# One 128-key, 64-query score matmul per chunk in HGRN2's six lower levels, in place of two of 64 by 32

## The chip, the cores and the metric

The kernel runs on one core of a Trainium2 chip. The metric is device time of one execution in microseconds (us). Three runs of the kernel before took 2519.35, 2517.97 and 2510.12 us, median 2517.97. The execution that the profiler recorded took 2514.51 us, of which the trace spans 2512.7.

## The reference

One decoder layer over 2048 tokens of width 1024, in float32: RMSNorm, one wide input projection, three token mixers, gates, an output projection, a residual and a final norm. Only mixer A, HGRN2, is touched. It has 4 heads of 128 key and 128 value channels, and works in chunks of 64 tokens. Within a chunk

```
b = jnp.cumsum(gb, axis=2)
diff = b[:, :, :, None, :] - b[:, :, None, :, :]
decay = jnp.exp(jnp.where(causal, diff, -jnp.inf))
scores = jnp.einsum('bhtk,bhsk,bhtsk->bhts', qb, kb, decay)
o = (jnp.einsum('bhts,bhsv->bhtv', scores, vb)
     + jnp.einsum('bhtk,bhkv->bhtv', qb * jnp.exp(b), state))
```

The decay between key s and query t differs for each of the 128 channels, so the scores are not one plain product of Q and K.

## The kernel before

The tokens are taken in four blocks of 512 (`block`, s = 0 to 3), each of which is four chunks of 128 tokens in this kernel (`NT` = 4, indexed c). A block projects the normed tokens onto all columns of `w_in`: every float32 product is written as three matmuls of 128x512 (L101, L102, L103; high times high, high times low, low times high), with weights streamed from DRAM. In the first block the weights are also split into high and low parts (L86 on ScalarE, L87 on VectorE) and kept in DRAM; later blocks load the kept parts. Around these projections the mixers run: `unit_a(h)` for each of 4 HGRN2 heads, `unit_b` for DeltaNet, `unit_c` for attention, and `merge` for each branch.

`unit_a` builds the decayed scores by levels. Tokens of a chunk are rows 0 to 127. At level lv (0 to 6) the chunk falls into blocks of 2h tokens, h = 2^lv, and each block into a lower and an upper half. The scores between queries of upper halves and keys of lower halves of the same block are exact products of Q and K as they stand at this level. After that Q of the upper halves is multiplied by the decay total of the lower half (L411), and K of the lower halves by that of the upper half (L412); so Q and K are right for the next level. A level's steps are these:

- TensorE: the score matmuls of the four chunks into one PSUM bank `sp` (L402 for levels 0 to 5, L406 for level 6). They read Q and K.
- VectorE: L411 writes Q and L412 writes K in place, so both wait for the score matmuls, and the matmuls of the next level wait for both.
- VectorE: L415 copies from `sp` to the score tile `SD` where the mask `amask` of this level is set (copy_predicated). `SD` has 128 rows (keys) by 64 columns (queries of the same 64-token half) for each chunk.
- GpSimd: L425 multiplies pairs of decay totals for the next level.

Queries and keys in different 64-token halves of a chunk meet only at level 6 (L406). So levels 0 to 5 need, for each chunk, two 64 by 64 squares, and of each only the 32 queries in upper halves. Before, each square has a matmul of its own: 64 keys are the stationary operand (64 columns of the array), 32 queries stream, and `tile_position=(0, g * 64)` puts the half g into columns 64g to 64g + 63 of the array and partitions 64g to 64g + 63 of the bank. A level has 8 such calls; each float32 call shows in the trace as two weight loads and two matmuls, so a level is 16 and the kernel (4 blocks, 4 heads, 6 levels: 96 groups) is 1536.

L406 (level 6) also uses a column tile, and is not changed. After level 6 the score tile goes to `ST` (L421, L422 on ScalarE), L429 and L434 are transposes, and L444 to L446 apply the scores and the state. L338 are transposes of the head before (`y_gate`), which fall among the first levels of the next head. L121 is the last step of a SiLU (`gate_ct`), on VectorE.

The instructions of an engine run in the order of its program. A scheduler lays the engines' programs out ahead of the run: it sets the projection matmuls (L101 to L103) between the score groups of two levels. PSUM banks for scores come from a pool of two per head parity (`bank(ct)`).

Of the kernel before, what the change touches and what calls it, by code (L numbers as in the profile page):

```python
# [20 lines left out]
P = 128  # L21
# [3 lines left out]
NT = TB // P  # L25
# [26 lines left out]
def _trunk(tc, S, a, out):  # L52
# [9 lines left out]
    V, A, G, T = nc.vector, nc.scalar, nc.gpsimd, nc.tensor  # L62
# [9 lines left out]
    def bank(tag="d", w=None):  # L72
        return ps.tile([P, 512], F32, name="ps_" + tag, tag=tag, bufs=4 if tag == "d" else 2)
# [44 lines left out]
    def silu2(dst, src, tag="tr"):  # L118
        th = sb.tile([P, src.shape[-1]], F32, name="th", tag=tag, bufs=2)
        last_act[0] = A.activation(th, src, AF.Tanh, scale=0.5).ins  # L120
        V.scalar_tensor_tensor(dst, th, 1.0, src, op0=ALU.add, op1=ALU.mult)  # L121
# [93 lines left out]
    amask = const.tile([P, 6, 32], U8, name="amask", tag="amask")  # L215
# [25 lines left out]
    def row_scale(so, c, eps):  # L241
        G.tensor_tensor(so[:, c:c + 1], so[:, c:c + 1], eps, op=ALU.add)
        G.tensor_tensor(so[:, c:c + 1], so[:, c:c + 1], mhalf4[:, 0:1], op=ALU.pow)
# [70 lines left out]
    def block(s, hH, hL, last=None):  # L314
        t0 = s * TB

        def proj_ct(idx):
            p = bank()
            mm_ct(p, a["wct"][idx], hH, hL, KT)
            return p  # L320

        def gate_ct(idx):
            pg = proj_ct(idx)
            gt = sb.tile([P, TB], F32, name="gt", tag="gt")
            silu2(gt, pg)
            return gt
# [5 lines left out]
        def y_gate(o, so, gt, nw, ct):  # L332
            pt = bank(ct)
            with tc.issue_after(last_act[0]), tc.issue_after(last_mm[0]):
                for c in range(NT):
                    A.activation(o[:, c, :], o[:, c, :], AF.Copy, scale=so[:, c:c + 1])
                for c in range(NT):
                    T.transpose(pt[:, c * P:(c + 1) * P], o[:, c, :], ident)  # L338
            V.scalar_tensor_tensor(gt, pt, nw, gt, op0=ALU.mult, op1=ALU.mult)

        def y_split(yT, h, gt):
            A.copy(yT[0][:, h, :], gt)  # L342
            V.tensor_tensor(yT[1][:, h, :], gt, yT[0][:, h, :].bitcast(F32), op=ALU.subtract)  # L343
# [25 lines left out]
        def unit_a(h):  # L369
            ct = "c%d" % (h % 2)  # L370
            hs = slice(h * P, (h + 1) * P)
            qk = sb.tile([P, 2, TB], F32, name="qk", tag="qk")
            Q, K = qk[:, 0, :], qk[:, 1, :]
            pf = proj_ct(4 + h)
            F = sb.tile([P, TB], F32, name="F", tag="w0")
            A.activation(F, pf, AF.Sigmoid)
            A.activation(K, pf, AF.Sigmoid, scale=-1.0)
            A.activation(F, F, AF.Identity, scale=omlb[:, h:h + 1], bias=lb[:, h:h + 1])
            A.activation(K, K, AF.Copy, scale=omlb[:, h:h + 1])
            pq = proj_ct(h)  # L380
            silu2(Q, pq)
            gt = gate_ct(8 + h)
            prod = sb.tile([P, TB], F32, name="prod", tag="w1")
            G.tensor_tensor(prod, Q, K, op=ALU.mult)
            V.tensor_tensor(Q, Q, F, op=ALU.mult)
            ST = sb.tile([P, NT, P], F32, name="ST", tag="w2")
            G.memset(ST[64:P, :, 0:64], 0.0)
            SD = sb.tile([P, NT, 64], F32, name="SD", tag="xf")
            G.memset(SD, 0.0)
            tots = sb.tile([P, TB], F32, name="tots", tag="w3")  # L390
            tot = F
            off = 0
            for lv in range(7):
                hh = 1 << lv
                nb = 64 >> lv
                v5 = lambda t: t.rearrange("p (c b two h) -> p c b two h", c=NT, b=nb, two=2, h=hh)
                sp = bank(ct)
                qv, kv = v5(Q), v5(K)
                for c in range(NT):
                    if lv < 6:  # L400
                        for g in range(2):
                            T.matmul(sp[g * 64:g * 64 + 64, c * 32:(c + 1) * 32], K[:, c * P + g * 64:c * P + g * 64 + 64],  # L402
                                     qv[:, c, g * nb // 2:(g + 1) * nb // 2, 1, :], start=True, stop=True,
                                     tile_position=(0, g * 64))
                    else:
                        T.matmul(sp[0:64, c * 64:(c + 1) * 64], kv[:, c, 0, 0, :], qv[:, c, 0, 1, :],  # L406
                                 start=True, stop=True, tile_position=(0, 0))
                tv = tot.rearrange("p (c b two) -> p c b two", c=NT, two=2)
                te = tv[:, :, :, 0:1].broadcast_to([P, NT, nb, hh])
                to = tv[:, :, :, 1:2].broadcast_to([P, NT, nb, hh])  # L410
                V.tensor_tensor(qv[:, :, :, 1, :], qv[:, :, :, 1, :], te, op=ALU.mult)  # L411
                V.tensor_tensor(kv[:, :, :, 0, :], kv[:, :, :, 0, :], to, op=ALU.mult)  # L412
                if lv < 6:
                    n2 = nb // 2
                    V.copy_predicated(  # L415
                        SD.rearrange("p c (b two h) -> p c b two h", b=n2, two=2, h=hh)[:, :, :, 1, :],
                        amask[:, lv, :].rearrange("p (o b h) -> p o b h", o=1, b=n2).broadcast_to([P, NT, n2, hh]),
                        sp[:, :P].rearrange("p (c b h) -> p c b h", c=NT, b=n2))
                else:
                    for r in (0, 64):  # L420
                        A.copy(ST[r:r + 64, :, r:r + 64], SD[r:r + 64])  # L421
                    A.copy(ST[0:64, :, 64:P], sp[0:64, 0:256].rearrange("p (c h) -> p c h", c=NT))  # L422
                nt_ = tots[:, off:off + NT * nb]
                off += NT * nb
                G.tensor_tensor(nt_.rearrange("p (c b) -> p c b", c=NT), tv[:, :, :, 0], tv[:, :, :, 1], op=ALU.mult)  # L425
                tot = nt_
            cp = bank(ct)
            for c in range(NT):
                T.transpose(cp[:, c * P:(c + 1) * P], prod[:, c * P:(c + 1) * P], ident)  # L429
            cc = sb.tile([P, NT], F32, name="cc", tag="cc")  # L430
            V.tensor_reduce(cc, b3(cp), axis=mybir.AxisListType.X, op=ALU.add)
            kp = bank(ct)
            for c in range(NT):
                T.transpose(kp[:, c * P:(c + 1) * P], K[:, c * P:(c + 1) * P], ident)  # L434
            KTt = sb.tile([P, TB], F32, name="KTt", tag="w4")
            A.copy(KTt, kp)
            o = b3(prod)
            st = stA[h]
            so = sb.tile([P, NT], F32, name="so", tag="so")
            for c in range(NT):  # L440
                cs = slice(c * P, (c + 1) * P)
                op = bank(ct)
                vv = vA[:, c, hs]
                T.matmul(op[:, 0:P], ST[:, c, :], vv, start=True, stop=False)  # L444
                T.matmul(op[:, 0:P], Q[:, cs], st, start=False, stop=True)
                T.matmul(op[:, P:2 * P], KTt[:, cs], vv, start=True, stop=True)  # L446
                V.scalar_tensor_tensor(st, st, tot[:, c:c + 1], op[:, P:2 * P], op0=ALU.mult, op1=ALU.add)
                V.scalar_tensor_tensor(o[:, c, :], vv, cc[:, c:c + 1], op[:, 0:P], op0=ALU.mult, op1=ALU.add)
                junk = sb.tile([P, P], BF16, name="junk", tag="junk")
                A.activation(junk, o[:, c, :], AF.Square, accum_out=so[:, c:c + 1])  # L450
                row_scale(so, c, epsa)

            def fin(yT):
                y_gate(o, so, gt, norma, ct)
                y_split(yT, h, gt)
            return fin
# [317 lines left out]
        if last:  # L774
            last()
        yA = new_y()
        f0 = unit_a(0)
        if s == 0:
            bias_rows()
        f1 = unit_a(1)  # L780
        if s == 0:
            bias_spread()
        f0(yA)
        proj_k()
        f2 = unit_a(2)
        if s == 0:
            bias_load()
# [126 lines left out]
```

## Time and profile before

| what | value |
|---|---|
| runs (median; lowest to highest) | 2517.97 us; 2510.12 to 2519.35 |
| profiled execution | 2514.51 us, span 2512.7 us |
| TensorE matmul busy | 97% of the span, 13658 matmuls |
| VectorE, ScalarE, GpSimd busy | 47%, 35%, 17% |
| granted TensorE clock, mean | 0.984 |
| DMA queues' share of 16 engines | 55% for the main one |

Busy is the time in which at least one instruction of the engine is in progress. Consecutive matmuls overlap: one takes about 0.39 us from its start to its end, and the next starts before that. So the pace is read from the differences of starts, not from durations. A weight load (PEld) is an instruction of its own, and runs beside matmuls.

### The profile page before, as it was taken

To read this page: it belongs to the slowest core of one execution; us is meant where nothing else is said; L and a number is where in the kernel's file an instruction comes from. 1 tells how busy PE (TensorE), PEld (TensorE's weight loads), DVE (VectorE), ACT (ScalarE), POOL (GpSimd) and SP (SyncE) were. 2 spreads that over 40 slices of the span, in tenths; PEclk is the share of its full clock that TensorE was granted. 3 is DMA by queue.
4 is the path that set the end of the run, shared out by engine and by line. 5 is a ranking of instruction groups with operands and counts; after the bars stand their busy time and mean duration, and the time that the engine had idled before them with its cause. 6 is when DMAs were issued, how large, how long until landed. Compare 5 with 4: busy or idle time off the path is not lost. (4 is left out here: it accounts for less than half of the span.)

```text
span 2512.7 us, 37478 instructions
## 1 busy us (share of the span) xinstructions
PE 2428.6 (97%) x13658; PEld 1946.4 (77%) x13658; DVE 1170.9 (47%) x3188; ACT 869.2 (35%) x2288; POOL 434.2 (17%) x821
## 2 busy tenths in 40 slices
PE   8999998999999999899999999989999999998998
PEld 7777776778877777678887877767888787876886
DVE  5666575465345535524214553551322455455321
ACT  5454344444334313323223422332322342233221
POOL 3221011211222101111112210111111221111111
PEclk9999998999999999999999999999999999999999
DMA  7756673769944455264774455425566354442555
GB/s 244 247 193 224 221 260 96 241 221 336 299 134 130 154 161 158 83 208 148 247 218 127 139 156 165 146 88 193 167 228 210 122 155 149 160 150 87 176 193 175
DMA packets 193156, 452.84 MB, mean 180 GB/s; under 512 B 52243, under 2 KB 70588, under 8 KB 192844
## 3 DMA queue, kind: packets, MB, share of 16 engines
q1 hardware_dynamic: 192972, 450.45, 55.3%
q8 instruction: 108, 1.77, 0.3%
q14 instruction: 76, 0.62, 0.1%
HBM read 348.81 MB, written 103.14 MB: 180 GB/s over the span
## 5 line engine op out<-in xcount | busy, mean ns | idle before, releaser
L101 PE MATMUL ps_d<-hH,wHL 128*128 128x512 f32 x1952 | 785.6, 402 | 4.1 <-DVE mm L700 2.2
L102 PE MATMUL ps_d<-hL,wHL 128*128 128x512 f32 x1952 | 783.5, 401 | 0.0
L103 PE MATMUL ps_d<-hH,wHL 128*128 128x512 f32 x1952 | 779.9, 400 | 0.7 <-DVE wHL L87 0.7
L101 PEld LDWEIGHTS ps_d<-hH,wHL 128*128 128x128 f32 x1952 | 369.4, 189 | 77.5 <-DVE mm L700 3.9
L103 PEld LDWEIGHTS ps_d<-hH,wHL 128*128 128x128 f32 x1952 | 369.3, 189 | 71.8 <-issue 1.8
L102 PEld LDWEIGHTS ps_d<-hL,wHL 128*128 128x128 f32 x1952 | 369.4, 189 | 68.0 <-issue 1.7
L87 DVE TENSOR_TENSOR wHL<-wraw,wHL 128x512 fp32r<-128x512 f32 (+1 forms) x194 | 130.6, 677 | 93.3 <-ACT wHL L86 91.2
L362 POOL TENSOR_TENSOR msum<-msum,gth 128x512 f32<-128x512 f32 x64 | 88.6, 1387 | 443.6 <-DVE gth L361 443.6
L101 PE MATMUL ps_d<-yH,wHL 128*128 128x512 f32 x384 | 155.3, 406 | 5.8 <-ACT yH L342 3.7
L86 ACT CAST wHL<-wraw 128x512 fp32r<-128x512 f32 (+1 forms) x194 | 113.7, 590 | 130.9 <-PE ps_d L103 80.8
L103 PE MATMUL ps_d<-yH,wHL 128*128 128x512 f32 x384 | 154.9, 403 | 0.0
L102 PE MATMUL ps_d<-yL,wHL 128*128 128x512 f32 x384 | 153.8, 401 | 0.1
L352 ACT ACTIVATE gth<-ps_d 128x512 f32<-128x512 f32 x96 | 57.3, 597 | 256.9 <-PE ps_d L103 256.1
L361 DVE SCALAR_TENSOR_TENSOR gth<-gth,ps_d 128x512 f32<-128x512 f32 x64 | 43.9, 687 | 184.9 <-PE ps_d L103 177.4
L169 PE MATMUL ps_d<-wHL,mH 128*128 128x512 f32 x256 | 99.7, 391 | 1.3 <-DMA wHL<-kept 1.3
L502 DVE SCALAR_TENSOR_TENSOR qkB<-raw,convw,qkB 128x512 f32<-128x512 f32 x96 | 71.7, 746 | 61.2 <-ACT qkB L500 59.9
L170 PE MATMUL ps_d<-wHL,mH 128*128 128x512 f32 x256 | 99.6, 389 | 0.0
L171 PE MATMUL ps_d<-wHL,mL 128*128 128x512 f32 x256 | 99.5, 389 | 0.0
L101 PEld LDWEIGHTS ps_d<-yH,wHL 128*128 128x128 f32 x384 | 73.0, 191 | 21.8 <-ACT yH L342 4.6
L102 PEld LDWEIGHTS ps_d<-yL,wHL 128*128 128x128 f32 x384 | 73.6, 192 | 15.9 <-DVE yL L343 1.7
L103 PEld LDWEIGHTS ps_d<-yH,wHL 128*128 128x128 f32 x384 | 73.5, 191 | 15.2 <-issue 0.5
L402 PEld LDWEIGHTS ps_c<-qk 128*64 128x64 f32 x1536 | 52.6, 137 | 33.3 <-issue 20.4
(281 smaller groups left out, 3761.0 us busy)
## 6 DMA issues: line engine op xcount, KB each, us to landing
wHL<-kept SPq DMA_DIRECT2D x486, 512.0 KB, 3.6
kept<-wHL SPq DMA_DIRECT2D x162, 512.0 KB, 4.0
wraw<-in_wct_dram SPq DMA_DIRECT2D x122, 256.0 KB, 3.7
wHL<-kept SPq DMA_DIRECT2D x32, 324.0 KB, 4.1
xT<-in_xT_dram SPq DMA_DIRECT2D x32, 256.0 KB, 4.6
xs<-in_x_dram SPq DMA_DIRECT2D x32, 256.0 KB, 4.4
rt<-in_x_dram SPq DMA_DIRECT2D x32, 256.0 KB, 4.6
out_dram<-rt SPq DMA_DIRECT2D x32, 256.0 KB, 4.0
```

Source lines behind the costliest of these rows:

```text
L86: A.copy(w[:, 0, :n], raw[:, :n])
L87: V.tensor_tensor(w[:, 1, :n], raw[:, :n], w[:, 0, :n].bitcast(F32), op=ALU.subtract)
L101: T.matmul(p, wh[:, ks], rh[kt], start=(kt == 0), stop=False)
L102: T.matmul(p, wh[:, ks], rl[kt], start=False, stop=False)
L103: last_mm[0] = T.matmul(p, wl[:, ks], rh[kt], start=False, stop=(kt == nk - 1)).ins
L169: T.matmul(pj[j][:, :n], lh[kt][:, js], wh, start=(kt == 0), stop=False)
L170: T.matmul(pj[j][:, :n], lh[kt][:, js], wl, start=False, stop=False)
L171: T.matmul(pj[j][:, :n], ll[kt][:, js], wh, start=False, stop=(kt == KT - 1))
L352: A.activation(th, gp, AF.Tanh, scale=0.5)
L362: G.tensor_tensor(m, m, th, op=ALU.add)
L402: T.matmul(sp[g * 64:g * 64 + 64, c * 32:(c + 1) * 32], K[:, c * P + g * 64:c * P + g * 64 + 64], qv[:, c, g * nb // 2:(g + 1) * nb // 2, ...
L502: V.scalar_tensor_tensor(dst, raw[:, j:j + TB], convw[:, ti, j:j + 1], dst, op0=ALU.mult, op1=ALU.add)
```

## The change

For levels 0 to 5 each chunk has one score matmul: all 128 keys are the stationary operand (128 columns of the array, no column tile), and the 64 queries of upper halves of both 64-token halves stream. The bank then also holds products of keys of one half and queries of the other, which nothing reads. A level has 4 calls, 8 weight loads and 8 matmuls; `sp` uses 256 columns instead of 128. As the wanted columns differ between the two partition halves, L415 becomes two predicated copies of 64 partitions each. Level 6 is unchanged.

```diff
                 for c in range(NT):
                     if lv < 6:
-                        for g in range(2):
-                            T.matmul(sp[g * 64:g * 64 + 64, c * 32:(c + 1) * 32], K[:, c * P + g * 64:c * P + g * 64 + 64],
-                                     qv[:, c, g * nb // 2:(g + 1) * nb // 2, 1, :], start=True, stop=True,
-                                     tile_position=(0, g * 64))
+                        T.matmul(sp[:, c * 64:(c + 1) * 64], K[:, c * P:(c + 1) * P], qv[:, c, :, 1, :],
+                                 start=True, stop=True)
                     else:
...
                 if lv < 6:
                     n2 = nb // 2
-                    V.copy_predicated(
-                        SD.rearrange("p c (b two h) -> p c b two h", b=n2, two=2, h=hh)[:, :, :, 1, :],
-                        amask[:, lv, :].rearrange("p (o b h) -> p o b h", o=1, b=n2).broadcast_to([P, NT, n2, hh]),
-                        sp[:, :P].rearrange("p (c b h) -> p c b h", c=NT, b=n2))
+                    for r in (0, 64):
+                        V.copy_predicated(
+                            SD[r:r + 64].rearrange("p c (b two h) -> p c b two h", b=n2, two=2, h=hh)[:, :, :, 1, :],
+                            amask[r:r + 64, lv, :].rearrange("p (o b h) -> p o b h", o=1, b=n2).broadcast_to([64, NT, n2, hh]),
+                            sp[r:r + 64, 0:256].rearrange("p (c g b h) -> p g c b h", c=NT, g=2, b=n2)[:, r // 64])
```

In the changed file the lines after the edit move: its L401 is the score matmul (before L402), L409 and L410 are the updates of Q and K (before L411, L412), L414 the predicated copies (before L415), and L404 the level-6 matmul (before L406).

TensorE's program in the third block, head 0, levels 2 to 4, before (`ps_d` is a projection's bank, `ps_c` with a number one level's score bank, `wHL` streamed weights, `hH` and `hL` the normed tokens' parts, `qk` the tile of Q and K; xN is the number of calls):

```order
L402 MATMUL ps_c_12284<-qk 64x32 x8
L103 MATMUL ps_d<-hH,wHL 128x512
L101 MATMUL ps_d<-hH,wHL 128x512
L102 MATMUL ps_d<-hL,wHL 128x512
L103 MATMUL ps_d<-hH,wHL 128x512
L402 MATMUL ps_c_12297<-qk 64x32 x8
L101 MATMUL ps_d<-hH,wHL 128x512
```

and with the change:

```order
L401 MATMUL ps_c_12134<-qk 128x64 x4
L103 MATMUL ps_d<-hH,wHL 128x512
L101 MATMUL ps_d<-hH,wHL 128x512
L102 MATMUL ps_d<-hL,wHL 128x512
L103 MATMUL ps_d<-hH,wHL 128x512
L401 MATMUL ps_c_12144<-qk 128x64 x4
L101 MATMUL ps_d<-hH,wHL 128x512
```

Here nothing but the group itself changes: four projection matmuls stand between two levels, as before.

VectorE's program at the same place, before (`tots` are the decay totals, `SD` the scores):

```order
L411 TENSOR_TENSOR qk<-qk,tots 128x32x8
L412 TENSOR_TENSOR qk<-qk,tots 128x32x8
L415 COPY_PREDICATED SD<-amask,ps_c_12297 128x16x8
L411 TENSOR_TENSOR qk<-qk,tots 128x16x16
```

and with the change:

```order
L409 TENSOR_TENSOR qk<-qk,tots 128x32x8
L410 TENSOR_TENSOR qk<-qk,tots 128x32x8
L414 COPY_PREDICATED SD<-amask,ps_c_12144 64x16x8 x2
L409 TENSOR_TENSOR qk<-qk,tots 128x16x16
```

The second copy stands behind the updates of Q and K, and ahead of those of the next level.

TensorE's program between levels 0 and 1 of head 1 in the third block, before (L338 are the transposes of head 0's output):

```order
L402 MATMUL ps_c_12510<-qk 64x32 x8
L101 MATMUL ps_d<-hH,wHL 128x512
L102 MATMUL ps_d<-hL,wHL 128x512
L103 MATMUL ps_d<-hH,wHL 128x512
L338 MATMUL ps_c_12654<-ident,prod 128x128
L101 MATMUL ps_d<-hH,wHL 128x512
L338 MATMUL ps_c_12654<-ident,prod 128x128
L102 MATMUL ps_d<-hL,wHL 128x512
L338 MATMUL ps_c_12654<-ident,prod 128x128
L103 MATMUL ps_d<-hH,wHL 128x512
L402 MATMUL ps_c_12523<-qk 64x32 x8
L338 MATMUL ps_c_12654<-ident,prod 128x128
```

and with the change:

```order
L401 MATMUL ps_c_12348<-qk 128x64 x4
L101 MATMUL ps_d<-hH,wHL 128x512
L102 MATMUL ps_d<-hL,wHL 128x512
L103 MATMUL ps_d<-hH,wHL 128x512
L338 MATMUL ps_c_12474<-ident,prod 128x128 x2
L101 MATMUL ps_d<-hH,wHL 128x512
L338 MATMUL ps_c_12474<-ident,prod 128x128
L102 MATMUL ps_d<-hL,wHL 128x512
L338 MATMUL ps_c_12474<-ident,prod 128x128
L401 MATMUL ps_c_12358<-qk 128x64 x4
```

All four transposes now stand ahead of the level-1 group, and one projection matmul fewer.

## Rows read from the trace of the kernel before

**Rows 1.** The page: span, busy time of each engine.

```profile
span 2512.7 us, 37478 instructions
PE 2428.6 (97%) x13658; PEld 1946.4 (77%) x13658; DVE 1170.9 (47%) x3188; ACT 869.2 (35%) x2288; POOL 434.2 (17%) x821
```

**Rows 2.** One line, L402: durations (min/median/max, ns), and its waits.

```profile
L402 PEld LDWEIGHTS ps_c<-qk x1536: 132/138/139, 62.9 to 2029.0; 128*64 128x64 f32 x192
L402 PE MATMUL ps_c<-qk x1536: 222/223/244, 62.9 to 2029.1; 128*64 128x32 f32 x192
  DVE qk L411: 83.4, 90
```

**Rows 3.** Timeline of PE (start, duration), third block: 21 projection matmuls, first and last.

```profile
1308.77 0.39 PE L101 MATMUL ps_d<-hH,wHL 128*128 128x512 f32 x1
...
1313.30 0.39 PE L103 MATMUL ps_d<-hH,wHL 128*128 128x512 f32 x1
```

**Rows 4.** Timeline of PE, third block, head 0, levels 1 to 3.

```profile
1316.02 0.66 PE L402 MATMUL ps_c<-qk 128*64 128x32 f32 x16
...
1317.41 0.39 PE L102 MATMUL ps_d<-hL,wHL 128*128 128x512 f32 x1
1317.73 0.66 PE L402 MATMUL ps_c<-qk 128*64 128x32 f32 x16
...
1319.45 0.66 PE L402 MATMUL ps_c<-qk 128*64 128x32 f32 x16
```

**Rows 5.** Timeline of PE and PEld, end of the same head: groups without column tiles.

```profile
1329.17 0.40 PE L445 MATMUL ps_c<-stA,qk 128*128 128x128 f32 x2
...
1331.47 0.41 PE L445 MATMUL ps_c<-stA,qk 128*128 128x128 f32 x2
...
1330.67 0.30 PEld L444 LDWEIGHTS ps_c<-vA,ST 128*128 128x128 f32 x2
1330.89 0.19 PEld L102 LDWEIGHTS ps_d<-hL,wHL 128*128 128x128 f32 x1
```

**Rows 6.** Timeline of PE, third block: 128-column weights with 16 streamed columns.

```profile
1404.16 0.29 PE L480 MATMUL ps_c<-gg,triu 128*128 128x16 f32 x2
1404.52 0.63 PE L338 MATMUL ps_c<-ident,prod 128*128 128x128 f32 x4
```

**Rows 7.** Timeline, third block, head 0, level 6 and its first users.

```profile
1324.59 0.68 PE L406 MATMUL ps_c<-qk 128*64 128x64 f32 x8
1324.97 0.81 ACT L421 COPY ST<-SD 64x256 f32<-64x256 f32 x2
...
1326.92 0.38 PE L444 MATMUL ps_c<-vA,ST 128*128 128x128 f32 x2
```

**Rows 8.** Timeline of DVE at levels 2 and 3 of rows 4.

```profile
1318.44 0.42 DVE L411 TENSOR_TENSOR qk<-qk,tots 128x256 f32<-128x256 f32 x1 [0.60 <-PE ps_c L402]
1318.78 0.42 DVE L412 TENSOR_TENSOR qk<-qk,tots 128x256 f32<-128x256 f32 x1
1319.12 0.28 DVE L415 COPY_PREDICATED SD<-amask,ps_c 128x128 f32<-128x128 uint8 x1
```

**Rows 9.** Timeline of DVE and PEld, DeltaNet: a load that waits for VectorE.

```profile
2291.61 0.35 DVE L642 TENSOR_SCALAR vn<-ps_c,cols 128x128 f32<-128x128 f32 x1 [0.22 <-PE ps_c L640]
2292.01 0.30 PEld L644 LDWEIGHTS ps_c<-vn,KD 128*128 128x128 f32 x2 [0.18 <-DVE vn L642]
```

**Rows 10.** Timeline of DVE, head 1, level 0.

```profile
1340.24 0.43 DVE L411 TENSOR_TENSOR qk<-qk,F 128x256 f32<-128x256 f32 x1 [2.62 <-PE ps_c L402]
...
1341.18 0.42 DVE L412 TENSOR_TENSOR qk<-qk,F 128x256 f32<-128x256 f32 x1
```

**Rows 11.** Groups by line, shapes apart (busy us, mean ns, idle before).

```profile
L415 DVE COPY_PREDICATED SD<-amask,ps_c 128x128 f32<-128x128 uint8 x96 | 32.6, 339 | 0.0
L666 DVE TENSOR_TENSOR kL<-ps_d,kH 64x512 fp32r<-64x512 f32 x16 | 11.0, 687 | 0.4
L750 DVE TENSOR_TENSOR rt<-ps_d,rt 128x512 f32<-128x512 f32 x32 | 21.4, 688 | 81.8 <-PE ps_d L171 81.8
```

## The prediction

> **What bounds the kernel.** I read the page's busy shares first, then the changed line by itself, then the order of time around it on TensorE and on VectorE. TensorE is busy for 97% of the span, the next engine for 47% [rows 1]. What lengthens or shortens TensorE's program by itself therefore moves the end by as much; what happens on VectorE counts only where TensorE comes to wait for it. The reader should see in the line's own rows that the busy time is no price: 1536 matmuls of 223 ns lie over one another, and the rows do not say what a group costs [rows 2]. The price is in the starts.
>
> **What a group costs now.** A projection matmul follows the one before in (1313.30 - 1308.77) / 20 = 0.2265 us [rows 3]. From one score group to the next with four of them between it is (1319.45 - 1316.02) / 2 = 1.715 us [rows 4]. So a group takes 1.715 - 4 x 0.2265 = 0.81 us of TensorE. Its 16 matmuls start within 0.66 - 0.223 = 0.44 us of each other, 29 ns apart on the mean; the other 0.37 us is entry and exit. At the entry the group starts 0.32 us after the projection matmul ahead of it (1317.73 - 1317.41) [rows 4], where 0.2265 would do: some 0.09 us are lost before a column tile. The rest is lost behind it.
>
> The Trainium skill says the same of the entry ("TensorEngine Tiling (Array Packing)", Key Properties): to change the tiling mode drains the engine. The 0.09 us agrees with that, and the change does away with it.
>
> **What a group will cost.** There are 8 matmuls, each with a load of 128 columns, no column tile, and 64 streamed columns. No row before has just this. Three rows lie around it.
>
> - With 128-column loads and 128 streamed columns: between two L445 stand six matmuls of L445, L446 and L444 and two projections, and (1331.47 - 1329.17) / 2 - 2 x 0.2265 = 0.70 us for six, 0.116 each with entry and exit. The loads alone follow each other at 1330.89 - 1330.67 = 0.22 us for two, 0.11 each [rows 5]. For 8: 0.88 by the loads, 0.93 by the whole.
> - With 128-column loads and only 16 streamed columns: four matmuls of L480 and L481 take 1404.52 - 1404.16 = 0.36 us, 0.09 each [rows 6]. For 8: 0.72. So short streams hardly help: the load sets the pace.
> - With 64-column loads and 64 streamed columns: one matmul's 0.222 taken off, (0.68 - 0.222) / 7 = 0.065 each [rows 2, 7]. For 8 with 0.03 at the ends: 0.55.
>
> I take 0.90, since the loads of 128 columns are what all rows with such loads are paced by, and the nearest group in length (six) gives 0.116 with its ends. Per group 0.90 - 0.81 = +0.09 us, and 96 groups make **+8.6 us**. The bounds are 0.72 (-8.6 us) and 0.93 (+11.5 us). In words: half as many matmuls, but two loads of 64 columns, one in each half of the array, go through in 2 x 29 = 58 ns, and one load of 128 takes 110. What the mode switches give back (0.3 us a group) is a little less than what the loads cost.
>
> The Trainium skill has a rule that speaks against the change too ("TensorE: Matmul & The Clock Gate", LDWEIGHTS (loading the stationary operand)): the time of a load goes with its columns, about one per 1.2 GHz cycle, so 107 ns for 128. The load rows agree (0.11). By that figure 8 loads take 0.86 us, and the term would be +5 us instead of +8.6.
>
> **The chain through VectorE.** The loads of the next level wait for L412's K, and L411 waits for the group's last matmul. Now: L411 starts 1318.44 - 1317.73 = 0.71 us after the group's first matmul, that is 0.27 after the start of its last; L412 starts 0.34 later and takes 0.42 [rows 4, 8]. It ends at 1.47, and the next group starts at 1.715: 0.24 us to spare less the hand-over. That from VectorE to a load is 2292.01 - (2291.61 + 0.35) = 0.05 us [rows 9].
>
> With the change the last matmul starts at 7 x 0.11 = 0.77. With 0.28 for the longer stream L411 starts at 1.05 and L412 ends at 1.05 + 0.34 + 0.42 = 1.81. The load starts at 1.86 and its matmul can run at 1.97. TensorE has done the group and four projections at 0.90 + 0.91 = 1.81. So it waits 0.16 to 0.17 us, and in part this is a load of 0.11 that was hidden under a projection before and now lies bare. In the changed program 34 gaps ahead of an L401 group hold four projections and nothing else (4 in the first block, 10 in each other): **+5.8 us**. Eight more such gaps end at level 6; L404 still loses 0.09 at its entry, until 1.90, which covers the load's 1.86. Gaps of six or more projections have 0.4 us or more of cover, and there I put nothing.
>
> The gap behind level 0 is long on VectorE too, as L121 stands between L411 and L412: from L411's start to L412's end 1341.18 + 0.42 - 1340.24 = 1.36 us [rows 10]. The matmul can run at 1.05 + 1.36 + 0.16 = 2.57. TensorE gets there at 0.90 + 7 x 0.2265 = 2.49, or, where five projections and four transposes stand there (0.11 each), at 2.47. Sixteen heads, 0.08 to 0.10 each: **+1.4 us**.
>
> **The copies.** One copy of 128 partitions takes 339 ns on the mean [rows 11]. Half the partitions do not make it shorter: 64x512 takes 687 ns and 128x512 takes 688 (L666, L750) [rows 11]. So the second copy adds 96 x 0.34 = 33 us to VectorE, which sits behind L412 and is done by about 2.4 us after the group's first matmul; the next L411 is not wanted before 1.97 + 1.05. While TensorE runs the next group, this hides it; I put nothing on the path. If that cover were gone, it would be 0.3 us in each of the 34 short gaps, 10 us. ScalarE's L421 needs level 5's second copy, at most 0.3 us later than now; its two copies end at 1325.78 now, and L444, which wants `ST`, starts at 1326.92 [rows 7].
>
> **Sum.** 8.6 + 5.8 + 1.4 = 15.8 us on the profiled execution's 2514.51 gives 2530.3. That execution lies 3.5 us below the runs' median, so I say 2531.
>
> **Rivals.**
> - *The waits do not come*: the group takes 0.90, but the chain is shorter than I make it (the last matmul ends sooner, or the scheduler's order leaves more). For it: nothing waits there now. Against: 0.24 us of spare is less than the 0.34 by which L411 moves back. It would be +8.6, 2523 us. Chance 0.20.
> - *The loads follow at 0.09*, as in the four of L480 and L481: the group takes 0.72, -8.6 us. But then L412 ends at 0.63 + 0.28 + 0.76 = 1.67, the matmul can run at 1.83, and TensorE is there at 0.72 + 0.91 = 1.63: 34 x 0.20 and some 2 us at level 0 eat the gain, and it is about 2515. Chance 0.10.
> - *Faster: the number of matmuls counts*, and the load is no bound with 64 streamed columns. Then the pace is L406's, 0.065, and the group 0.55: 96 x -0.26 = -25 us. L412 ends at 0.455 + 0.28 + 0.76 = 1.50 and the matmul could run at 1.66, TensorE is there at 1.46: +6.8. Net -18, 2496 us. It decides from a load pace under some 0.085 us. Against it stand rows 5 and 6. Chance 0.07. The Trainium skill has a rule that leads here ("TensorEngine Tiling (Array Packing)", Instruction Overhead): a matmul has about 60 cycles of fixed cost, so one column takes as long as 60, and a small dimension should not be split. It would hold if loads were free; the trace shows them bare between short matmuls.
> - *The second copy lands on the path* where VectorE has other work between levels (L339, L343, or the weight splits L87 in the first block): up to 10 us more, 2541. Chance 0.08.
>
> **How the numbers follow.** My forecast has 0.55, with 2526 to 2537 as its own range. The range from 2510 to 2545 takes in the low load pace at the bottom and the copies at the top, with the runs' scatter of some 4 us to either side; what it leaves out is the faster rival and a small tail above. A measurement of this kernel can tell about 0.5% (12.6 us) from no change. Slower by more than that: nine tenths of the forecast and the copy rival, 0.58. Within it: the rest of the forecast, hidden waits and the 0.09 pace, 0.35. Faster: 0.07.
>
> **What would show it.** L401 should have 768 loads and matmuls, with 0.11 us between their starts; a pace under 0.09 would prove me wrong. The matmul after a group should start 0.11 after the group's last, with no 0.32 at the entry. In the gaps of four projections TensorE should wait for L410, 0.1 to 0.2 us, in some 34 places, and the list of waits should have an L401 row on VectorE of about 6 us or a little less. L414 should take 0.29 to 0.43 each, twice per level, with no wait behind it. VectorE's busy time should rise by 33 us.

## The result, and the profile after

The changed kernel is slower, by a little: median 2540.05 us over 6 runs (2533.72 to 2549.31) against 2521.66 for the kernel before on the same chip (6 runs, 2510.12 to 2527.98). The ratio is 1.0072, with a 95% interval from 1.0044 to 1.0099. Its profiled execution took 2533.72 us, 19.2 more than that of before. The page, which answers to [rows 1]:

```profile
span 2531.9 us, 36045 instructions
PE 2447.3 (97%) x12890; PEld 1983.4 (78%) x12890; DVE 1214.1 (48%) x3284; ACT 869.0 (34%) x2288; POOL 437.2 (17%) x821
```

TensorE has 768 matmuls fewer and is busy for 18.7 us longer. VectorE has 96 instructions more and 43 us more of busy time. The changed line by itself answers to [rows 2]: the count and the durations (min/median/max, ns), then for how long and how often its engine waited for L410, and L409 for it.

```profile
L401 PEld LDWEIGHTS ps_c<-qk x768: 186/192/193, 63.1 to 2044.4; 128*128 128x128 f32 x192
L401 PE MATMUL ps_c<-qk x768: 217/275/324, 63.3 to 2044.5; 128*128 128x64 f32 x192
L401 PEldq EVENT_SEMAPHORE  x35: 51/51/51, 63.0 to 2043.2; - x35
...
  DVE qk L410: 8.7, 33
...
  DVE qk L409: 62.6, 63
```

Now the pace, in the timeline of TensorE in the third block, head 0 (start, duration). Level 0's group, which has nothing to wait for:

```profile
1322.03 0.39 PE L103 MATMUL ps_d<-hH,wHL 128*128 128x512 f32 x1
1322.26 1.00 PE L401 MATMUL ps_c<-qk 128*128 128x64 f32 x8
1323.07 0.48 PE L101 MATMUL ps_d<-hH,wHL 128*128 128x512 f32 x1
1323.39 0.39 PE L102 MATMUL ps_d<-hL,wHL 128*128 128x512 f32 x1
```

The entry is 1322.26 - 1322.03 = 0.23, so the 0.09 lost before a column tile is gone. The group's last matmul starts at 1322.26 + 1.00 - 0.27 = 1322.99; the projection behind it follows 0.08 later, where 0.11 was forecast, and the next one 0.32 after that. From the projection ahead to the second one behind are 1.36 us; two projections at 0.227 taken off, the group costs 0.91. I measured in this way, from the starts, every group that has a projection ahead of it and two behind. Before, 84 such groups cost 0.798 us on the mean. After, the 16 first groups of a head cost 0.899, and the 21 with six projections ahead 0.903.

Levels 1 and 2 of the same head, with a gap of four projections between them, and what VectorE does there:

```profile
1324.80 1.08 PE L401 MATMUL ps_c<-qk 128*128 128x64 f32 x8
...
1325.92 0.43 DVE L409 TENSOR_TENSOR qk<-qk,tots 128x256 f32<-128x256 f32 x1 [0.44 <-PE ps_c L401]
1326.26 0.42 DVE L410 TENSOR_TENSOR qk<-qk,tots 128x256 f32<-128x256 f32 x1
1326.47 0.39 PE L102 MATMUL ps_d<-hL,wHL 128*128 128x512 f32 x1
1326.71 0.92 DVE L414 COPY_PREDICATED SD<-amask,ps_c 64x128 f32<-64x128 uint8 x2
1326.80 0.97 PEld L401 LDWEIGHTS ps_c<-qk 128*128 128x128 f32 x8 [0.37 <-issue]
1326.83 1.08 PE L401 MATMUL ps_c<-qk 128*128 128x64 f32 x8
1327.71 0.48 PE L103 MATMUL ps_d<-hH,wHL 128*128 128x512 f32 x1
1328.03 0.40 PE L101 MATMUL ps_d<-hH,wHL 128*128 128x512 f32 x1
```

L410 ends at 1326.68. The last projection started at 1326.47, and the group could have started at 1326.70; its first load comes at 1326.80, and the matmul behind it at 1326.83. From 1326.47 to 1328.03, less two projections, the group costs 1.11: 0.20 more than without a wait. The eight loads take (0.97 - 0.19) / 7 = 0.111 us each, start to start. Both copies stand behind L410 and reach to 1327.63, beside the group.

How much of the 19.2 us lies here is read from a stretch that holds nearly the same work in both profiles: in the second block, from the first score group of head 0 to the last of head 3. One row for each (us, busy time and count of each engine, granted clock, DMA share, GB/s), before and after:

```profile
695.09:788.97 93.88, 93.77 (x769) 72.73 (x768) 48.11 (x128) 34.11 (x83) 20.83 (x52) 1.00 0.41 125
```

```profile
698.12:796.55 98.43, 98.43 (x586) 81.36 (x584) 57.38 (x149) 33.62 (x82) 20.63 (x52) 1.00 0.39 119
```

The stretch is 4.55 us longer, at the same clock. In the four blocks it is 3.66, 4.55, 4.57 and 4.56 us, together 17.3. Besides the score matmuls the work differs by one projection matmul: in each block 264 stand in the stretch after and 263 before. Four times 0.227 taken off, the groups and their waits make 16.4 us. The other 2.8 us of the 19.2 are differences of both signs outside these stretches; I put them down to nothing.

### The profile page after: what moved, and what is told of

Read it like the earlier page. It is cut to its first block, busy times and chain, and to the rows that moved or that the text cites. A ratio compares the mean times of both kernels' runs of the same rounds, so it can differ in the third digit from the quotient of the medians.

```text
span 2531.9 us, 36045 instructions
## 1 busy us (share of the span) xinstructions
PE 2447.3 (97%) x12890; PEld 1983.4 (78%) x12890; DVE 1214.1 (48%) x3284; ACT 869.0 (34%) x2288; POOL 437.2 (17%) x821
## 5 line engine op out<-in xcount | busy, mean ns | idle before, releaser
L401 PEld LDWEIGHTS ps_c<-qk 128*128 128x128 f32 x768 | 96.0, 191 | 18.3 <-DVE qk L410 8.7
L401 PE MATMUL ps_c<-qk 128*128 128x64 f32 x768 | 100.2, 273 | 0.0
L101 PEld LDWEIGHTS ps_d<-yH,wHL 128*128 128x128 f32 x384 | 73.1, 191 | 21.6 <-ACT yH L342 4.6
```

The lines of the kernel that those rows point to most:

```text
L101: T.matmul(p, wh[:, ks], rh[kt], start=(kt == 0), stop=False)
L401: T.matmul(sp[:, c * 64:(c + 1) * 64], K[:, c * P:(c + 1) * P], qv[:, c, :, 1, :], start=True, stop=True)
```

## The experiments

All were timed beside the kernel before on the same chip; those of one set share its runs. My theory is the prediction's: the loads of 128 columns set the group's pace, the longer group makes the chain through VectorE late in short gaps, and the copies cost nothing. The rivals: the copies carry the loss, or the streamed columns do.

**The change again.** Same kernel.

> The changed kernel itself, beside the kernels of this call. Theory (loads of 128 columns, plus VectorE's chain that no longer fits under four projections): 1.006 to 1.008 of the time before, as measured once already. A group costs 0.90 us where nothing waits, against 0.80 before, and 1.04 to 1.10 behind a gap of four projections. Rival (the second predicated copy is what costs): the same time, but kernel e1 shows it and e2 loses it.

Measured: 2536.25 against 2515.89, ratio 1.0082 [1.0060, 1.0103]. The loss is there again, at the same size.

**The copies alone.** The matmuls of before, and its copy split in two:

```diff
+                    for r in (0, 64):
                     V.copy_predicated(
-                        SD..., amask[:, lv, :]..., sp[:, :P]...)
+                        SD[r:r + 64]..., amask[r:r + 64, lv, :]..., sp[r:r + 64, :P]...)
```

> The kernel before with its two 64-key matmuls per chunk, and only the predicated copy split into two of 64 partitions. Theory: VectorE busy +33 us, TensorE's groups unchanged at 0.80 us, time 1.000 of before (within 0.15%, 4 us). Rival (the copies are on the path): +8 to +12 us, 1.003 to 1.005.

Measured: 2518.34, ratio 1.0012 [0.9994, 1.0031]. The busy times of the page, and the copies in the groups by line (busy us, mean ns, idle before), which answer to [rows 1, 11]:

```profile
PE 2432.1 (97%) x13658; PEld 1948.3 (77%) x13658; DVE 1210.6 (48%) x3284; ACT 867.8 (34%) x2288; POOL 437.8 (17%) x821
```

```profile
L416 DVE COPY_PREDICATED SD<-amask,ps_c 64x128 f32<-64x128 uint8 x192 | 65.7, 342 | 5.0
```

A copy of 64 partitions takes 342 ns on the mean, as one of 128 did. VectorE is busy for 40 us more, and the score groups cost 0.797, as before. So the copies are hidden, as far as this comparison can tell: at most 0.3% by its interval.

**The matmuls alone.** The merged matmul with one copy of 128 partitions, which takes the first half's query columns for both halves of the partitions:

```diff
-                    for r in (0, 64):
-                        V.copy_predicated(SD[r:r + 64]..., sp[r:r + 64, 0:256]...[:, r // 64])
+                    V.copy_predicated(SD..., sp[:, 0:256]...[:, 0])
```

> The merged 128-key, 64-query matmul, but one predicated copy of all 128 partitions, which takes the columns of the first half's queries for both halves (the scores of the second half of each 64+64 pair are left wrong). Theory: loads and waits of the changed kernel stay, so 1.006 to 1.008 of before; groups behind four projections still 1.04 to 1.10 us. Rival (copies): 1.003 or less.

Measured: 2535.71, ratio 1.0076 [1.0060, 1.0092]. By line, and in the waits (us in total, times, longest):

```profile
L413 DVE COPY_PREDICATED SD<-amask,ps_c 128x128 f32<-128x128 uint8 x96 | 32.4, 338 | 0.0
```

```profile
PEld ps_c L401 <- DVE qk L410: 8.2, 27, 0.3
```

With 33 us of copies taken away the loss is all there: groups behind four projections cost 1.060 on the mean (32 of them), the others 0.90 in the median, of which the eight behind level 0 with seven projections cost 0.95 to 1.02. With the run before, this settles that the matmuls alone make the kernel slower.

**K before Q.** I took the loads to wait for K alone. Then K's update ahead of Q's would give back most of the wait:

```diff
-                V.tensor_tensor(qv[:, :, :, 1, :], qv[:, :, :, 1, :], te, op=ALU.mult)
                 V.tensor_tensor(kv[:, :, :, 0, :], kv[:, :, :, 0, :], to, op=ALU.mult)
+                V.tensor_tensor(qv[:, :, :, 1, :], qv[:, :, :, 1, :], te, op=ALU.mult)
```

> The changed kernel with the update of K issued ahead of the update of Q; TensorE's program has the same gaps. The loads wait for K alone, the matmuls for both, so with K first the load of 0.11 us is hidden again while VectorE updates Q. Theory: in the 34 gaps of four projections the group costs 0.11 us less (about 0.93 to 0.99 instead of 1.04 to 1.10), -3.5 to -4 us against the changed kernel, 0.0015 of the time. Rival (the groups' extra cost there is not a wait for VectorE but an effect of the array): no change of the 1.04 to 1.10.

Measured: 2540.71, ratio 1.0098 [1.0074, 1.0121]; groups behind four projections cost 1.080. Nothing is given back, and I was wrong. The timeline of VectorE and the loads, where L409 is now K's update and L410 Q's:

```profile
1327.79 0.43 DVE L409 TENSOR_TENSOR qk<-qk,tots 128x256 f32<-128x256 f32 x1 [0.32 <-PE ps_c L401]
1328.13 0.42 DVE L410 TENSOR_TENSOR qk<-qk,tots 128x256 f32<-128x256 f32 x1
1328.66 0.97 PEld L401 LDWEIGHTS ps_c<-qk 128*128 128x128 f32 x8 [0.37 <-issue]
1328.69 1.08 PE L401 MATMUL ps_c<-qk 128*128 128x64 f32 x8
```

K is done at 1328.22, and the load that reads it starts at 1328.66, which is 0.11 behind the end of Q's update. So in this program the load starts only when both operands of its matmul call are there. Of the 30 gaps that can be measured 18 now have an instruction more on the load queue, for 12 in the changed kernel (told below, with the waits); each kind costs what it cost there, 1.10 and 1.04, and the mean rises from 1.064 to 1.080 by the mix.

**Two loads of 128.** Each chunk's 128 keys are loaded for each half's 32 queries, so the matmuls are as many as before and stream as many columns, without column tiles:

```diff
-                        T.matmul(sp[:, c * 64:(c + 1) * 64], K[:, c * P:(c + 1) * P], qv[:, c, :, 1, :],
-                                 start=True, stop=True)
+                        for g in range(2):
+                            T.matmul(sp[:, c * 64 + g * 32:c * 64 + g * 32 + 32], K[:, c * P:(c + 1) * P],
+                                     qv[:, c, g * nb // 2:(g + 1) * nb // 2, 1, :], start=True, stop=True)
```

> All 128 keys stationary, no column tile, but two matmuls of 32 queries per chunk instead of one of 64: the same columns streamed, twice the loads of 128 columns (1536). Theory (the load is the pace): 16 x 0.111 us, a group costs about 1.79 us instead of 0.90; with the waits behind short gaps as in the changed kernel the time is 1.038 to 1.044 of before, +85 us on the changed kernel. Rival (streamed columns are the pace): the group stays at 0.90 and the time at 1.007.

Measured: 2613.36 against 2521.50, ratio 1.0374 [1.0341, 1.0407]. The timeline of TensorE:

```profile
718.16 0.39 PE L101 MATMUL ps_d<-hH,wHL 128*128 128x512 f32 x1
718.40 1.94 PE L402 MATMUL ps_c<-qk 128*128 128x32 f32 x16
720.18 0.48 PE L102 MATMUL ps_d<-hL,wHL 128*128 128x512 f32 x1
720.49 0.40 PE L103 MATMUL ps_d<-hH,wHL 128*128 128x512 f32 x1
```

The group costs 720.49 - 718.16 - 2 x 0.227 = 1.88 here, and 1.79 to 1.80 where nothing waits: with 0.90 for eight matmuls, 0.111 for each one more, at half the streamed columns. Against the kernel before, the same number of matmuls with the same streams costs 1.80 in place of 0.80. The ratio is just below what was expected: by the groups, 0.88 us more on the mean, the run would be 85 us longer than the changed kernel, and the profiled executions differ by 78. It spent 67 us at the lower granted clock (0.50), the changed kernel 82, which gives back up to 8 us.

**Half the stream.** The merged matmul with its load of 128 keys, but only the first half's 32 queries streamed, which both copies then read:

```diff
-                        T.matmul(sp[:, c * 64:(c + 1) * 64], K[:, c * P:(c + 1) * P], qv[:, c, :, 1, :],
+                        T.matmul(sp[:, c * 64:c * 64 + 32], K[:, c * P:(c + 1) * P], qv[:, c, 0:nb // 2, 1, :],
...
```

> The merged matmul with 128 keys, but only the 32 queries of the first half stream; both predicated copies read these columns (scores of the second half left wrong). Theory (the load is the pace): 0.111 us from matmul to matmul as with 64, a group of 0.90 us where nothing waits, time 1.006 to 1.008 of before. Rival (streamed columns or a fixed cost plus columns): pace under 0.09, group 0.72 or less, time 1.000 or less.

Measured: 2538.23, ratio 1.0079 [1.0050, 1.0108]. The timeline of TensorE:

```profile
700.10 0.39 PE L103 MATMUL ps_d<-hH,wHL 128*128 128x512 f32 x1
700.33 0.97 PE L401 MATMUL ps_c<-qk 128*128 128x32 f32 x8
701.14 0.48 PE L101 MATMUL ps_d<-hH,wHL 128*128 128x512 f32 x1
701.46 0.40 PE L102 MATMUL ps_d<-hL,wHL 128*128 128x512 f32 x1
```

The group costs 701.46 - 700.10 - 2 x 0.227 = 0.91, as with 64 columns. So between 32 and 64 streamed columns the pace does not change; with the run before, it goes with the loads.

**Two heads at once.** If entry and exit of a column tile cost 0.37 us a group, two column-tiled groups in touch should share them. The matmuls are those of before; two heads run their levels side by side, and the second head's group is issued behind the first's:

```diff
-                for c in range(NT):
+                def score(...):
+                    for c in range(NT):
...
+                yield score
...
+        def pair_a(h):
+            gs = [unit_a(h), unit_a(h + 1)]
+            for _ in range(7):
+                f0, f1 = [next(g) for g in gs]
+                f1()
+                with tc.issue_after(last_sc[0]):
+                    f0()
+            return [next(g) for g in gs]
```

> The kernel before with its column-tiled score matmuls, but two heads worked at once, the score groups of both behind one another on TensorE (some pairs still have one projection matmul between them). Theory: entry to and exit from a column tile cost 0.37 us per group in the kernel before, and are paid once for two groups that touch: the second group of a pair costs about 0.46 us instead of 0.80. About 30 pairs touch: -10 us, 0.996 of before, if the new order makes no other waits; behind level 6 the state updates of both heads now stand with no projections between them, which may cost as much again. Rival (no cost of entry and exit): groups in touch still cost 0.80 each.

Measured: 2521.32 against 2521.50, ratio 1.0009 [0.9993, 1.0026]. The timeline of TensorE, a pair in touch, and the waits of TensorE:

```profile
1352.02 0.39 PE L101 MATMUL ps_d<-hH,wHL 128*128 128x512 f32 x1
1352.33 1.12 PE L403 MATMUL ps_c<-qk 128*64 128x32 f32 x32
1353.39 0.50 PE L102 MATMUL ps_d<-hL,wHL 128*128 128x512 f32 x1
1353.72 0.39 PE L103 MATMUL ps_d<-hH,wHL 128*128 128x512 f32 x1
```

```profile
PE ps_c L338 <- ACT prod L336: 14.0, 17, 2.7
```

The pair costs 1353.72 - 1352.02 - 2 x 0.227 = 1.25 us for two, 0.63 each against 0.80. I counted 34 such pairs. At 14 more a projection got between the two groups; from the projection ahead of such a pair to the second one behind it, less three projections, it costs 1.59, as much as two groups before. By the pairs that is 34 x 0.35 = 11.9 us gained. A new wait takes it back: with two heads' ends together the transposes L338 stand behind ScalarE for 14.0 us, 0.7 before. The two make +1.4 us, and the ratio says +2.3, in an interval that takes in no change.

**Pairs, with the wait mended.** Against the last kernel, the order of the two groups alternates by level, and the transposes move behind the next head's projections:

```diff
-                f1()
+                fs[(lv + 1) % 2]()
                 with tc.issue_after(last_sc[0]):
-                    f0()
+                    fs[lv % 2]()
...
-        f2, f3 = pair_a(2)
+        f2, f3 = levels(g2, g3)
         with tc.issue_after(last_act[0]):
             gates_b()
-        f2(yA)
         f0 = unit_b(0)
+        f2(yA)
```

> The kernel before with two heads worked at once, the order of the two score groups changed from level to level so that 41 of 48 pairs stand behind one another on TensorE, and the output transposes of the first two heads set behind the next head's projections. Theory: two groups in touch cost 1.254 us as measured in p2, against 2 x 0.80, so 41 x 0.35 = -14 us, and the 14 us in which p2's transposes waited for ScalarE are gone: 0.993 to 0.997 of before. Rival (something else of the pairing costs as much): 0.998 to 1.002.

Measured: 2550.30 against 2517.82, ratio 1.0130 [1.0111, 1.0149]: slower. Waits of TensorE, and three stretches around DeltaNet's first step in the second block (columns as above):

```profile
PE ps_c L607 <- DVE X L597: 15.6, 12, 2.6
...
PE ps_d L101 <- ACT yH L342: 10.2, 8, 1.7
```

```profile
873.00:893.00 20.00, 17.69 (x81) 13.82 (x81) 9.57 (x28) 8.47 (x36) 7.05 (x12) 0.91 0.43 131
893.00:913.00 20.00, 18.19 (x87) 14.78 (x86) 7.41 (x33) 1.35 (x3) 0.00 (x0) 1.00 0.70 205
913.00:933.00 20.00, 20.00 (x72) 12.38 (x72) 6.43 (x21) 2.45 (x8) 0.53 (x1) 0.50 0.19 63
```

The two waits were 8.5 and 3.7 us before, so they have grown by 13.6. After two stretches with TensorE busy for 17.69 and 18.19 of 20 us, the granted clock is 0.50, its lower level of 1.2 GHz, for a stretch in which TensorE is busy throughout. In the whole span it is at that level for 130 us, against 82 before. 48 us at half speed that would have been at full cost up to 24. With the waits this makes at most 37.6 us. In this run 36 pairs are in touch, not the 41 that were expected, and 12 have one to three projections between; the 36 give back some 12 us. So at most 25 us are accounted for, against a loss of 32.5; how the parts overlap, and what else there is, stays open. By the order of the program, projections that covered DeltaNet's waits before now stand elsewhere; that this is the cause I have not tested by itself.

**The same pairing with the merged matmul.** The last kernel with the score matmul and the copies of the change.

```diff
-                            for g in range(2):
-                                last_sc[0] = T.matmul(sp[g * 64:...], K[...], qv[...], ..., tile_position=(0, g * 64)).ins
+                            last_sc[0] = T.matmul(sp[:, c * 64:(c + 1) * 64], K[:, c * P:(c + 1) * P], qv[:, c, :, 1, :],
+                                                  start=True, stop=True).ins
...
```

> The same pairing with the merged 128-key, 64-query matmul of the changed kernel. Theory: without a column tile there is no entry or exit to share, so a pair costs 16 loads of 0.111 us, 1.79 us, against 1.254 in p5: +0.54 us in each of about 40 pairs, +22 us on p5, some 9 us of it above the kernel before's own groups; 1.002 to 1.006 of before. Rival (the changed kernel loses only by its waits behind short gaps): with both heads' groups to cover, no more than p5 and below 1.000.

Measured: 2577.17, ratio 1.0234 [1.0211, 1.0256], 27 us above the column-tiled pairs. The timeline of TensorE:

```profile
1382.18 0.40 PE L103 MATMUL ps_d<-hH,wHL 128*128 128x512 f32 x1
1382.41 1.90 PE L402 MATMUL ps_c<-qk 128*128 128x64 f32 x16
1384.12 0.48 PE L101 MATMUL ps_d<-hH,wHL 128*128 128x512 f32 x1
1384.43 0.39 PE L102 MATMUL ps_d<-hL,wHL 128*128 128x512 f32 x1
```

The pair costs 1384.43 - 1382.18 - 2 x 0.227 = 1.80 (median of all 1.795), twice 0.90. The merged matmul has no entry to and exit from a column tile to share, so where the column tiles are at their best it loses 0.54 us a pair, and not 2 x 0.10. As in the last kernel 36 pairs are in touch, which makes 19 us; the other 12 cost 1.80 for 1.59, 2.5 us more. That is 22 of the 27 us; the rest stays open. Both runs are at the lower clock for 130 us. No version here beat the kernel before.

## Why the prediction was right

The time came out at 2540 for 2531 in the medians, on 2521.66 where the forecast stood on 2518; by the profiled executions it is 19.2 us for 15.8. The forecast's last step is not clean: 15.8 us on the runs' median of 2517.97 is 2533.8, and 2531 takes in less than 1 of the 3.5 us by which the profiled execution lay below it. Term by term:

- **The load term** was the largest and a little too small: 0.90 - 0.80 = 0.10 us a group, 96 groups, 9.8 us, for +8.6. The group after was right to 0.01; the group before, 0.81 by one place, is 0.798 over 84. That the load is the cause and not the number of matmuls or their streams is shown by the two runs on it: twice the loads is 0.111 more for each, though the kernel before has as many matmuls in 0.80, and half the streamed columns is nothing. So the rival by the number of matmuls falls with its 0.065, and the one at 0.09 too. That 0.09 was misread from the starts of the matmuls in [rows 6], the first of which had its load made ahead, from 1403.93 on. The loads of the last two, in the timeline of the loads before, follow at 0.30 - 0.19 = 0.11:

```profile
1404.27 0.30 PEld L481 LDWEIGHTS ps_c<-gg,onesP 128*128 128x128 f32 x2
```

  Why two tiles are faster shows in the loads of head 0 in the third block before, a level with two column tiles and level 6 with one:

```profile
1317.73 0.55 PEld L402 LDWEIGHTS ps_c<-qk 128*64 128x64 f32 x16 [0.36 <-issue]
...
1324.59 0.54 PEld L406 LDWEIGHTS ps_c<-qk 128*64 128x64 f32 x8 [0.36 <-issue]
```

  Into one tile a load of 64 columns follows every (0.54 - 0.14) / 7 = 0.057 us, half of 0.111; into two tiles twice as many go in the same time. What a load of 64 columns outside a column tile costs, no run shows. The Trainium skill ("TensorE: Matmul & The Clock Gate", LDWEIGHTS (loading the stationary operand)) has 107 ns for a load of 128 columns; the trace has 111. The estimate of +5 by that figure was lower by these 4 ns a load, and by the group's ends. The Trainium skill's rule on the fixed cost of a matmul ("TensorEngine Tiling (Array Packing)", Instruction Overhead) led the other way here: half as many matmuls took 0.10 us longer a group.
- **The waits came**, so that the likeliest rival falls. Of the 34 short gaps 30 stand so that they can be measured: the groups behind them cost 1.064 on the mean, 0.16 above a group without a wait. 34 x 0.16 = 5.5 us, for +5.8. But two sentences of the step failed. The loads do not wait for K alone, as the run with K first shows; the chain came out right since K was the later of the two. The load in [rows 9] had shown it already: KD is the stationary operand of L644, and its load waits for vn, which streams. And the hand-over of 0.05 us holds only in part of the gaps. It does here, in the timeline of VectorE and the loads in the second block:

```profile
708.19 0.42 DVE L410 TENSOR_TENSOR qk<-qk,tots 128x256 f32<-128x256 f32 x1
...
708.66 0.97 PEld L401 LDWEIGHTS ps_c<-qk 128*128 128x128 f32 x8 [0.30 <-DVE qk L410]
```

  From 708.61 to 708.66 are 0.05, and such a group costs 1.04. In the gap shown first it is 0.12, and the group 1.11. There a semaphore instruction of 51 ns stands on TensorE's queue ahead of the load; it is the third row of the changed line above, 35 times. Of the 30 gaps 12 have it and cost 1.10 to 1.12, and the 18 without it cost 1.03 to 1.05. So where the hand-over was as I had it, the wait is 0.14 and not 0.17, and in the others it is 0.20. That the mean came out at 0.16 is in part luck.
- **The list of waits** has the row that I asked for, L410, with 8.7 us where I had about 6. It is weaker evidence than I took it for. It counts the time in which no load is in progress, and the kernel before had such rows too (8.5 us on L415, 26 times), where the groups cost no more than elsewhere. The starts of the matmuls show the price; the row does not.
- **Level 0**: thirteen gaps of seven projections can be measured, eight of them behind level 0; the groups behind these cost 0.94 to 1.02, 0.97 on the mean. That is about 0.07 each, and 1.1 us for sixteen if the other eight, which can't be measured, are alike, for +1.4.
- **Level 6** was covered, nearly: in seven of the eight short gaps the first matmul of L404 starts 0.35 or 0.36 us behind the last projection (710.71 - 710.35 in the second block), where a column tile starts 0.32 behind it in [rows 4]. In the eighth, in the first block, it starts 0.83 behind; there the updates of Q and K took 0.78 and 0.62 us. I had counted nothing here; it is about 0.7 us in all.
- **The copies** took 342 ns for the 0.29 to 0.43 forecast, and nothing on the path, as two runs show from either side. The rival that had them there falls. VectorE rose by 43 us for 33; 33.0 of it are the copies (65.6 us for 32.6 in [rows 11]). The other lines' durations together rise by only 1; about 5 us are overlap that is gone, as a copy used to start before the update of K had ended (1319.12, for 1318.78 + 0.42 = 1319.20 in [rows 8]) and in the gap shown starts behind it (1326.71 for 1326.68). The remaining 4 were not followed further.

The three terms that were forecast make 16.4 us as measured by the groups, and the stretches give 16.4 when the additional projection matmuls are taken off. That they agree so closely is chance, as level 6 is not among the three.

## What to carry to other kernels

When each short matmul has a load of its own, count the stationary columns that are loaded one behind another, not the matmuls: two column tiles load their 64 columns side by side, and merging them into one load of 128 gives that up. A longer group delays the engine that answers it, so check what cover the shortest gap has; here that was a third of the loss. Where column tiles cost something, it is at entry and exit, so put such groups next to each other, if the work between them isn't the cover of something else.

## What the runs showed of the hardware that was not expected

- With a load of 128 columns for each, matmuls of 32 and of 64 streamed columns follow each other at the same 0.111 us.
- Two column-tiled groups in touch cost 1.25 us, two apart 1.60: about 0.35 us is paid for each time TensorE goes into column tiles and out again.
- In these programs the load of a matmul call waits for both operands of the call, also for the one that it does not read: 0.11 us behind Q's update with K ready 0.33 earlier, and 0.05 behind vn in [rows 9].
- A semaphore instruction ahead of a load makes the hand-over from VectorE 0.12 us instead of 0.05.
- A predicated copy costs the same for 64 and 128 partitions, but its time depends on the level. In the run with the copies alone, the timeline of VectorE (two consecutive copies in a row, start and duration of both) shows levels 0, 1 and 2 of a head: 0.45 us a copy at the first two, 0.3 from the third on. The mean of 342 is made of both.

```profile
1314.42 0.91 DVE L416 COPY_PREDICATED SD<-amask,ps_c 64x128 f32<-64x128 uint8 x2
...
1316.33 0.91 DVE L416 COPY_PREDICATED SD<-amask,ps_c 64x128 f32<-64x128 uint8 x2
...
1318.07 0.62 DVE L416 COPY_PREDICATED SD<-amask,ps_c 64x128 f32<-64x128 uint8 x2
```
